# A Hymba-style inference step: RWKV chunk outputs in two rounds, two decoding states moved as whole tiles

## The chip, the core and the metric

One core of a Trainium2 chip runs the whole layer in one launch. The metric is the device time of one execution in microseconds. Every text below uses these names for the engines: PE (TensorE matmul), PEld (its weight loads), DVE (VectorE), ACT (ScalarE), POOL (GpSimd) and SP (SyncE, which here only issues DMAs). ACT and POOL issue DMAs too.

## What is computed

One decoder layer is applied to a prompt of 1024 tokens and to 8 decoding samples of one token each (N = 1032 columns). One input projection feeds four head groups, and a gated output projection and a layer norm close it:

```python
proj = jnp.einsum('ntd,de->nte', x, P['w_in'])
o_A, conv_n, S_A_n = _gdn_branch(...)      # causal convolution, then gated DeltaNet in chunks of 64
o_B, shift_n, S_B_n = _rwkv7_branch(...)   # RWKV-7 time mixing
o_C, k_n, v_n, lf_n = _fox_branch(...)     # attention with forget gates, 4096 cached tokens per sample
o_D, pool_n = _pool_branch(...)            # means over windows of 2, 4, 8 and 16
out = jnp.einsum('nte,ed->ntd', gated, P['w_out'])
y = _layernorm(ALPHA_DN * x + out, P['ln_g'], P['ln_b'])

# B, token by token:
S = S * w_t[:, :, None, :] + s_kk[..., :, None] * (kk_t * a_t)[:, :, None, :] + v_t[..., :, None] * k_t[:, :, None, :]
y_t = jnp.einsum('nhvk,nhk->nhv', S, r_t)
# A and D return the decoding states: the last 3 and the last 15 inputs of each sample
ext = jnp.concatenate([buf, u], axis=1);  new_buf = ext[:, T:]          # A: 3 rows kept
ext = jnp.concatenate([buf, u], axis=1);  new_buf = ext[:, -POOL_BUF:]  # D: 15 rows kept
```

## The kernel before, in words

Every wide product is three f32 matmuls on split operands (`mm3`, L308 to L310). The weights of the input projection (57 tiles of 128 columns) and of the output projection are loaded by ACT's queue as `raw`, split by ACT (`whi`, L302) and DVE (`wlo`, L303), and multiplied into three banks of 344 columns. The projection tiles run one after another on PE. Between them a list of generators ("fillers") is advanced at set rates: preparing the chunk operands, inverting triangular blocks (`invert`, L1176 and L1180), the recurrences, the decoding attention. A scheduler with a timeline of its own then writes the final order of every engine, so a shorter step in one place moves instructions after it. Each engine runs its own list in order.

Three places are touched.

- **`chain_b`** runs the RWKV recurrence over 16 chunks of 64 tokens, as a filler of the last projection tiles. Two heads share the 128 partitions, four such pairs (`hp`) lie side by side. A chunk has four steps on PE: `px` (L1320), `pz` (L1326), `pn` (L1332) and the output `py` (L1340, L1341). L1340 multiplies the old state over all 128 partitions into one half of the output partitions; L1341 adds the products of the chunk over the 64 partitions of one head. Both write 64 x 64 outputs. Each f32 product counts as two PE instructions. ACT then copies `py` into `byT` (L1343) and SP stores it.
- **`branch_d`** (pooling) runs as a filler after both recurrences, while decoding attention streams the cached keys (`dkv<-in_ck`, SP's queue, L924; used by PE at L994). It holds the 15 old rows of 8 samples in `dbf`, in rows of 16, puts the new input in column 15 (L711), sums the last `w` columns (L713) and stores columns 1 to 15 as `obuf` (L725). The same POOL queue stores and loads `dz`, the gate tile (L723, L716), of which there is one buffer.
- **`sample_a`** makes the decoding step of DeltaNet as a filler of the second output pass, beside cached values (`dkv<-in_cv`, L943; used at L1102). It holds the 3 old rows in `scb`, in rows of 4, puts the new input in column 3 (L1524), stores columns 1 to 3 as `oconv` (L1525) and convolves (L1531, L1533). The DMAs between are POOL's. A norm follows: ACT squares `so` into `sqk` (L1561), PE sums it (L1484).

Of the kernel before, what the change touches and what calls it, by code (L numbers as in the profile page):

```python
# [11 lines left out]
ALU = mybir.AluOpType  # L12
AX = mybir.AxisListType
# [166 lines left out]
class Kernel:  # L180
# [502 lines left out]
    def branch_d(self, pool):  # L683
        nc, O, I = self.nc, self.O, self.I
        pw = self.t(pool, [128, 4, 128], "dpw", bufs=1)
        nc.gpsimd.dma_start(pw, I["pw"])
        rc = self.t(pool, [128, 64], "drc", bufs=1)
        nc.gpsimd.dma_start(rc, I["rc"])
        bf = self.t(pool, [128, 4, 8, 16], "dbf", bufs=1)
        nc.gpsimd.dma_start(bf[:, :, :, 0:15], I["dbf"])  # L690
        for gi in range(4):
            w = 2 << gi
            u = self.t(pool, [128, 16 + N], "du", bufs=1)
            nc.gpsimd.memset(u[:, 0:16], 0.0)
            nc.gpsimd.dma_start(u[:, 16:], O["pj"][DU + gi])
            a = self.t(pool, [128, 16 + T], "da", bufs=1)
            b = self.t(pool, [128, 16 + T], "db", bufs=1)
            cur = u
            for s in range(gi + 1):
                d = 1 << s  # L700
                nxt = a if s % 2 == 0 else b
                if s < gi:
                    nc.gpsimd.memset(nxt[:, 0:16], 0.0)
                nc.vector.tensor_tensor(nxt[:, 16:], cur[:, 16:16 + T], cur[:, 16 - d:16 - d + T], op=ALU.add)
                cur = nxt
            nc.vector.tensor_tensor(cur[:, 16:32], cur[:, 16:32], rc[:, 16 * gi:16 * gi + 16], op=ALU.mult)
            yield 1
            po = self.t(pool, [128, 16 + N], "db" if gi % 2 == 0 else "da", bufs=1)[:, :N]
            nc.vector.scalar_tensor_tensor(po[:, :T], cur[:, 16:], 1.0 / w, u[:, 16:16 + T], op0=ALU.mult, op1=ALU.subtract)
            us = u[:, 16 + T:]  # L710
            nc.vector.tensor_copy(bf[:, gi, :, 15], us)  # L711
            sm = self.t(pool, [128, 8], "dsm", bufs=1)
            nc.vector.reduce_sum(sm, bf[:, gi, :, 16 - w:16], axis=AX.X)  # L713
            nc.vector.scalar_tensor_tensor(po[:, T:], sm, 1.0 / w, us, op0=ALU.mult, op1=ALU.subtract)
            z = self.t(pool, [128, N], "dz", bufs=1)
            nc.gpsimd.dma_start(z, O["pj"][DZ + gi])  # L716
            self.silu(z, self.t(pool, [128, 16 + N], "da" if cur is a else "db", bufs=1)[:, :N])
            for g in range(3):
                s = slice(g * G3, g * G3 + G3)
                ps = self.ps("b", (128, G3))  # L720
                nc.tensor.matmul(ps, lhsT=pw[:, gi], rhs=po[:, s], start=True, stop=True)
                nc.vector.scalar_tensor_tensor(z[:, s], ps, self.p("psc", gi), z[:, s], op0=ALU.mult, op1=ALU.mult)
            nc.gpsimd.dma_start(self.G[12 + gi], z)  # L723
            yield 1
        nc.gpsimd.dma_start(O["obuf"], bf[:, :, :, 1:16])  # L725


    def c_values(self, hp):
# [561 lines left out]
    def chain_b(self, **side):  # L1290
        nc, O = self.nc, self.O
        rows = [(slice(0, 64), slice(64, 128)), (slice(64, 128), slice(0, 64))]
        p3 = lambda a: a.rearrange("p (h i) -> p h i", i=64)
        with self.tc.tile_pool(reuse_waits="tile", name="chb", bufs=1, **side) as pool:

            def load(c):
                VZ = self.t(pool, [128, 4, 2, 64], "bvz", bufs=2)
                if c == 16:
                    return None, VZ, None
                op = self.t(pool, [128, 4, 512], "bop", bufs=2)  # L1300
                nc.sync.dma_start(op, self.BOP[c, :, :, 0:512])
                VS = self.t(pool, [128, 4, 2, 64], "bvs", bufs=2)
                for x in (VZ, VS):
                    for h, (_, t) in enumerate(rows):
                        nc.sync.dma_start(x[t, :, h], self.BOP[c, t, :, 512:576])
                return op, VZ, VS
            nxt = load(0)
            for h, (r, _) in enumerate(rows):
                nc.gpsimd.memset(nxt[1][r, :, h], 0.0)
            for c in range(16):  # L1310
                op, VZ, VS = nxt
                nxt = load(c + 1)
                Wv = op[:, :, 0:256].rearrange("p q (h a i) -> p q h a i", h=2, a=2)
                ZP = self.t(pool, [128, 4, 64], "bZP")
                for h, (r, _) in enumerate(rows):
                    nc.gpsimd.tensor_tensor(ZP[r], VZ[r, :, h], self.PC[r, :, c:c + 1].to_broadcast([64, 4, 64]), op=ALU.mult)
                px = self.ps("a", (128, 256))
                for hp in range(4):
                    for h, (r, _) in enumerate(rows):
                        nc.tensor.matmul(px[r, 64 * hp:64 * hp + 64], lhsT=Wv[:, hp, h, 0], rhs=VZ[:, hp, h], start=True, stop=True)  # L1320
                X = self.t(pool, [128, 4, 64], "bX")
                nc.vector.tensor_copy(X, p3(px))
                pz = self.ps("a", (128, 256))
                for hp in range(4):
                    for h, (r, _) in enumerate(rows):
                        nc.tensor.matmul(pz[r, 64 * hp:64 * hp + 64], lhsT=op[r, hp, 448:512], rhs=X[r, hp], start=True, stop=True)  # L1326
                nc.scalar.activation(VS[0:64, :, 0], p3(pz)[0:64], AF.Copy, scale=-1.0)
                nc.vector.tensor_scalar(VS[64:128, :, 1], p3(pz)[64:128], -1.0, None, op0=ALU.mult)
                pn = self.ps("a", (128, 256))
                for hp in range(4):  # L1330
                    for h, (r, _) in enumerate(rows):
                        nc.tensor.matmul(pn[r, 64 * hp:64 * hp + 64], lhsT=op[:, hp, 320 + 64 * h:384 + 64 * h], rhs=VS[:, hp, h],  # L1332
                                         start=True, stop=True)
                for h, (r, _) in enumerate(rows):
                    nc.vector.tensor_tensor(nxt[1][r, :, h], ZP[r], p3(pn)[r], op=ALU.add)
                py = self.ps("a", (128, 256))
                for hp in range(4):
                    o = slice(64 * hp, 64 * hp + 64)
                    for h, (r, _) in enumerate(rows):
                        nc.tensor.matmul(py[r, o], lhsT=VZ[:, hp, h], rhs=Wv[:, hp, h, 1], start=True, stop=False)  # L1340
                        nc.tensor.matmul(py[r, o], lhsT=VS[r, hp, h], rhs=op[r, hp, 256:320], start=False, stop=True)  # L1341
                yT = self.t(pool, [128, 4, 64], "byT", bufs=2)
                nc.scalar.copy(yT, p3(py))  # L1343
                nc.sync.dma_start(self.YB[:, :, 64 * c:64 * c + 64].rearrange("h p t -> p h t"), yT)
                yield True
            for h, (r, _) in enumerate(rows):
                nc.sync.dma_start(O["pBS"][:, r].rearrange("q p d -> p q d"), nxt[1][r, :, h])
# [154 lines left out]
    def sample_a(self, pool):  # L1502
        self.stag = "b"
        nc, I, O = self.nc, self.I, self.O
        pj, v_ = O["pj"], nc.vector
        f = lambda a: a.rearrange("p h b -> p (h b)")
        S = self.t(pool, [128, 4, 8, 64], "sS", bufs=1)
        nc.gpsimd.dma_start(S, I["sA"])
        cb = self.t(pool, [128, 12, 8, 4], "scb", bufs=1)
        nc.gpsimd.dma_start(cb[:, :, :, 0:3], I["cvb"])  # L1510
        xs = self.t(pool, [128, 12, 8], "sxs", bufs=1)
        for s in range(3):
            nc.gpsimd.dma_start(xs[:, 4 * s:4 * s + 4], pj[AT + s:AT + 16:4, :, T:].rearrange("h p b -> p h b"))
# [5 lines left out]
        for hh in range(2):  # L1519
            r = slice(64 * hh, 64 * hh + 64)  # L1520
            nc.gpsimd.dma_start(eg[r], self.gr[hh::2, T:].partition_broadcast(64))
            nc.gpsimd.dma_start(be[r], self.br[hh::2, T:].partition_broadcast(64))
        nc.scalar.activation(eg, eg, AF.Exp)
        v_.tensor_copy(cb[:, :, :, 3], xs)  # L1524
        nc.gpsimd.dma_start(O["oconv"], cb[:, :, :, 1:4])  # L1525
        cw = self.p("conv", 0, n=48).rearrange("p (c k) -> p c k", k=4)
        x = self.t(pool, [128, 12, 8], "sx", bufs=1)
        t = self.t(pool, [128, 12, 8], "st", bufs=1)
        for k in range(4):
            dst = x if k == 0 else t  # L1530
            v_.tensor_tensor(dst, cb[:, :, :, k], cw[:, :, k:k + 1].to_broadcast([128, 12, 8]), op=ALU.mult)  # L1531
            if k:
                v_.tensor_tensor(x, x, t, op=ALU.add)  # L1533
        self.silu(x, t)
        q, k, v = x[:, 0:4], x[:, 4:8], x[:, 8:12]
# [20 lines left out]
        o = self.t(pool, [128, 4, 8], "so", bufs=1)  # L1556
# [370 lines left out]
```

## Time and profile before

| | us |
|---|---|
| median of three runs (2544.55 to 2556.67) | 2548.86 |
| the profiled execution | 2552.96 |
| its span, first to last instruction | 2550.9 |
| PE busy in it | 2393.4 |
| DVE busy | 1371.8 |
| ACT busy | 941.1 |
| POOL busy | 305.7 |

The profile gives, for each engine, the time it was busy, what each wait ended on, and the clock that was granted to PE in a stretch (1.00 is 2.4 GHz, 0.50 is 1.2 GHz). PE instructions overlap in the pipeline, so the distance between the starts of two of them says more than the length of one. DMA share is the mean busy share of the core's 16 DMA engines.

### The profile page before, as it was taken

The numbers are of one execution on the slowest core, as the hardware profiler recorded it, in microseconds if no ns is written. First come the engines' busy times: TensorE is split into PE (matmuls) and PEld (weight loads), VectorE is DVE, ScalarE is ACT, GpSimd is POOL, SyncE is SP. The second block draws the span as 40 slices with busy tenths as digits, with TensorE's granted clock in tenths as the row PEclk, the third lists the DMA queues.
The fourth block names the chain that finished last, engine by engine and source line by source line (L and its number), as shares of the span: only waits on it lengthen the run. The fifth ranks groups of instructions, "written<-read, shape, count | busy, mean of one in ns | idle before, by whom it ended". The sixth has DMA issues, their size and how long they took to land.

```text
span 2550.9 us, 48595 instructions
## 1 busy us (share of the span) xinstructions
PE 2393.4 (94%) x18324; PEld 2101.0 (82%) x18324; DVE 1371.8 (54%) x2674; ACT 941.1 (37%) x1861; POOL 305.7 (12%) x416
## 2 busy tenths in 40 slices
PE   8999999999999999999999997999898799399984
PEld 8999999999979998887788775899655498268984
DVE  4675577687555574212122252555677543264598
ACT  5644444445444441111111121543565563010244
POOL 0000000000000000020111111100222212000065
PEclk9999999999999999889999998999999899799997
DMA  6243334555323357557777887653686767975322
GB/s 205 56 111 94 93 87 113 154 109 117 82 67 88 84 117 171 138 154 217 248 242 263 256 294 201 222 162 87 196 245 207 256 217 206 55 258 174 96 72 83
DMA packets 368740, 401.46 MB, mean 157 GB/s; under 512 B 203853, under 2 KB 227710, under 8 KB 367738
## 3 DMA queue, kind: packets, MB, share of 16 engines
q1 hardware_dynamic: 306418, 262.78, 36.9%
q10 hardware_dynamic: 50056, 101.60, 14.9%
q0 software_dynamic: 12032, 33.99, 4.3%
q8 instruction: 144, 2.36, 0.4%
q14 instruction: 90, 0.74, 0.1%
HBM read 314.56 MB, written 83.62 MB: 156 GB/s over the span
## 4 chain that ended last, share of the span: by engine, by line
PE 57%; DMA 9%; DVE 5%; issue 2%; ACT 1%; SPq 1%; another core or an unknown queue 0%; ACTq 0%; POOL 0%; DVEq 0%; POOLq 0%
PE pj L308 10%; PE pj L309 10%; PE pj L310 10%; PE o L308 4%; PE o L309 4%; PE o L310 3%; PE k L994 3%; DMA raw<-in_wo 3%; PE k L1102 2%; PE a L1341 1%; DMA dkv<-in_ck 1%; PE a L1340 1%; DVE y L1712 1%; DMA dkv<-in_cv 1%; DVE y L1711 1%
## 5 line engine op out<-in xcount | busy, mean ns | idle before, releaser
L308 PE MATMUL pj<-xh,wlo 128*128 128x344 f32 x2688 | 878.8, 328 | 15.8 <-DVE wlo L303 8.2
L309 PE MATMUL pj<-xl,whi 128*128 128x344 f32 x2688 | 875.1, 326 | 0.0
L310 PE MATMUL pj<-xh,whi 128*128 128x344 f32 x2688 | 869.8, 325 | 0.0
L308 PEld LDWEIGHTS pj<-xh,wlo 128*128 128x128 f32 x2688 | 511.4, 190 | 44.4 <-issue 18.2
L310 PEld LDWEIGHTS pj<-xh,whi 128*128 128x128 f32 x2688 | 511.7, 191 | 19.3 <-issue 16.1
L309 PEld LDWEIGHTS pj<-xl,whi 128*128 128x128 f32 x2688 | 512.0, 190 | 18.0 <-issue 12.3
L302 ACT CAST whi<-raw 128x256 fp32r<-128x256 f32 (+1 forms) x504 | 212.9, 424 | 772.9 <-PE pj L310 513.7
L303 DVE TENSOR_TENSOR wlo<-raw,whi 128x256 fp32r<-128x256 f32 (+1 forms) x504 | 225.3, 449 | 421.8 <-ACT whi L302 411.5
L308 PE MATMUL o<-gh,wlo 128*128 128x344 f32 x576 | 186.3, 328 | 4.7 <-ACT gh L1656 4.7
L309 PE MATMUL o<-gl,whi 128*128 128x344 f32 x576 | 186.8, 324 | 0.0
L310 PE MATMUL o<-gh,whi 128*128 128x344 f32 x576 | 186.2, 323 | 0.0
L308 PEld LDWEIGHTS o<-gh,wlo 128*128 128x128 f32 x576 | 108.7, 190 | 28.9 <-DVE y L1681 10.2
L309 PEld LDWEIGHTS o<-gl,whi 128*128 128x128 f32 x576 | 109.9, 191 | 4.7 <-issue 4.2
L310 PEld LDWEIGHTS o<-gh,whi 128*128 128x128 f32 x576 | 109.6, 190 | 3.3 <-issue 3.2
L994 PE MATMUL k<-dkv,dqb 128*32 128x256 f32 x1024 | 93.2, 400 | 17.4 <-DMA dkv<-in_ck 17.1
L365 ACT ACTIVATE stg<-pj 128x344 f32<-128x344 f32 x168 | 75.0, 457 | 90.4 <-PE pj L310 89.4
L1681 DVE TENSOR_TENSOR y<-y,o 128x344 f32<-128x344 f32 x96 | 48.1, 509 | 78.2 <-PE o L310 78.1
L1102 PE MATMUL k<-dkv,dpT 128*8 128x512 f32 x512 | 69.7, 620 | 4.6 <-DMA dkv<-in_cv 4.5
L858 DVE TENSOR_TENSOR cpl<-cpt,cph 128x512 fp32r<-128x512 f32 (+1 forms) x96 | 62.7, 667 | 19.5 <-ACT cph L857 18.9
L308 PE MATMUL o<-gh,wkl 128*128 128x392 f32 (+2 forms) x192 | 63.8, 332 | 0.5 <-DVE wkl L303 0.5
L994 PEld LDWEIGHTS k<-dkv,dqb 128*32 128x32 f32 x1024 | 27.7, 109 | 43.8 <-issue 30.6
L310 PE MATMUL o<-gh,wkh 128*128 128x392 f32 (+2 forms) x192 | 63.8, 332 | 0.0
(590 smaller groups left out, 3553.2 us busy)
## 6 DMA issues: line engine op xcount, KB each, us to landing
dkv<-in_ck SPq DMA_DIRECT2D x256, 256.0 KB
dkv<-in_cv SPq DMA_DIRECT2D x256, 256.0 KB
raw<-in_w ACTq DMA_DIRECT2D x228, 256.0 KB
out_pj<-stg ACTq DMA_DIRECT2D x33, 516.0 KB
bop<-bop SPq DMA_DIRECT2D x16, 1024.0 KB
raw<-in_wo ACTq DMA_DIRECT2D x64, 256.0 KB
aop<-aop SPq DMA_DIRECT2D x16, 768.0 KB
aop<-aost SPq DMA_DIRECT2D x40, 256.0 KB
```

The lines of the kernel that those rows point to most:

```text
L302: nc.scalar.copy(hi, raw)
L303: nc.vector.tensor_tensor(lo, raw, hi.bitcast(F32), op=ALU.subtract)
L308: nc.tensor.matmul(ps, lhsT=wlo, rhs=xh, start=start, stop=False)
L309: nc.tensor.matmul(ps, lhsT=whi, rhs=xl, start=False, stop=False)
L310: self.last = nc.tensor.matmul(ps, lhsT=whi, rhs=xh, start=False, stop=stop).ins
L365: self.nc.scalar.activation(dst[:, g * G3:g * G3 + G3], ps[g], func)
L858: nc.vector.tensor_tensor(pl[:, off:], pt[:, off:], ph[:, off:].bitcast(F32), op=ALU.subtract)
L994: nc.tensor.matmul(ps[32 * hp:32 * hp + 32], lhsT=qb[:, hp, b], rhs=kt[:, :, hp], start=b == 0, stop=b == 7)
L1102: mm = lambda i: nc.tensor.matmul(po[32 * i:32 * i + 8], lhsT=pTv[:, c, :, 4 * bg + i], rhs=t[i // 2][:, i % 2], start=False, stop=c == 31)
L1340: nc.tensor.matmul(py[r, o], lhsT=VZ[:, hp, h], rhs=Wv[:, hp, h, 1], start=True, stop=False)
L1341: nc.tensor.matmul(py[r, o], lhsT=VS[r, hp, h], rhs=op[r, hp, 256:320], start=False, stop=True)
L1681: nc.vector.tensor_tensor(y[:, s], y[:, s], ps[g], op=ALU.add)
```

## The change

In `chain_b` the two products of a chunk's output no longer alternate: first the eight products over 128 partitions, one for each `hp` and head, then the eight over 64. The first product of the chunk alone starts a fresh accumulation, the last alone ends it. In `branch_d` and `sample_a` the old state is loaded into a tile with no gaps, and the new state is made in a second tile by copies on DVE, so that both DMAs move a contiguous run per partition: 480 elements (obuf) and 288 (oconv) where single runs of 15 and of 3 elements stood. The window of 16 then needs one extra addition.

```diff
-        bf = self.t(pool, [128, 4, 8, 16], "dbf", bufs=1)
-        nc.gpsimd.dma_start(bf[:, :, :, 0:15], I["dbf"])
+        bf, bn = (self.t(pool, [128, 4, 8, 15], x, bufs=1) for x in ("dbf", "dbn"))
+        nc.gpsimd.dma_start(bf, I["dbf"])
+        nc.vector.tensor_copy(bn[:, :, :, 0:14], bf[:, :, :, 1:15])
...
-            nc.vector.tensor_copy(bf[:, gi, :, 15], us)
+            nc.vector.tensor_copy(bn[:, gi, :, 14], us)
...
-            nc.vector.reduce_sum(sm, bf[:, gi, :, 16 - w:16], axis=AX.X)
+            nc.vector.reduce_sum(sm, bn[:, gi, :, 15 - w:15] if w < 16 else bn[:, gi], axis=AX.X)
+            if w == 16:
+                nc.vector.tensor_tensor(sm, sm, bf[:, gi, :, 0], op=ALU.add)
...
-        nc.gpsimd.dma_start(O["obuf"], bf[:, :, :, 1:16])
+        nc.gpsimd.dma_start(O["obuf"], bn)
...
                 for hp in range(4):
-                    o = slice(64 * hp, 64 * hp + 64)
                     for h, (r, _) in enumerate(rows):
-                        nc.tensor.matmul(py[r, o], lhsT=VZ[:, hp, h], rhs=Wv[:, hp, h, 1], start=True, stop=False)
-                        nc.tensor.matmul(py[r, o], lhsT=VS[r, hp, h], rhs=op[r, hp, 256:320], start=False, stop=True)
+                        nc.tensor.matmul(py[r, 64 * hp:64 * hp + 64], lhsT=VZ[:, hp, h], rhs=Wv[:, hp, h, 1], start=hp == 0, stop=False)
+                for hp in range(4):
+                    for h, (r, _) in enumerate(rows):
+                        nc.tensor.matmul(py[r, 64 * hp:64 * hp + 64], lhsT=VS[r, hp, h], rhs=op[r, hp, 256:320], start=False, stop=hp == 3)
...
-        cb = self.t(pool, [128, 12, 8, 4], "scb", bufs=1)
-        nc.gpsimd.dma_start(cb[:, :, :, 0:3], I["cvb"])
+        cb, cn = (self.t(pool, [128, 12, 8, 3], x, bufs=1) for x in ("scb", "scn"))
+        nc.gpsimd.dma_start(cb, I["cvb"])
...
-        v_.tensor_copy(cb[:, :, :, 3], xs)
-        nc.gpsimd.dma_start(O["oconv"], cb[:, :, :, 1:4])
+        v_.tensor_copy(cn[:, :, :, 0:2], cb[:, :, :, 1:3])
+        v_.tensor_copy(cn[:, :, :, 2], xs)
+        nc.gpsimd.dma_start(O["oconv"], cn)
...
-            v_.tensor_tensor(dst, cb[:, :, :, k], cw[:, :, k:k + 1].to_broadcast([128, 12, 8]), op=ALU.mult)
+            v_.tensor_tensor(dst, cb[:, :, :, k] if k < 3 else xs, cw[:, :, k:k + 1].to_broadcast([128, 12, 8]), op=ALU.mult)
```

The first chunk output stands so in PE's list before (a row here is one product; its output tile, its operands, its output's shape):

```order
L1332 MATMUL a_10394<-bvs_10354,bop_10352 64x64 x7
L1340 MATMUL a_10405<-bop_10352,bvz_10351 64x64
L1341 MATMUL a_10405<-bop_10352,bvs_10354 64x64
L1340 MATMUL a_10405<-bop_10352,bvz_10351 64x64
L1341 MATMUL a_10405<-bop_10352,bvs_10354 64x64
...
L1176 MATMUL k_10871<-ivT_10864,ivD_10866 32x32 x12
L1320 MATMUL a_10498<-bvz_10361,bop_10362 64x64 x8
```

The pair of L1340 and L1341 stands there eight times. The same place in PE's list now (the lines are three to six further down in the file):

```order
L1335 MATMUL a_10394<-bvs_10354,bop_10352 64x64 x7
L1343 MATMUL a_10405<-bop_10352,bvz_10351 64x64 x8
L1346 MATMUL a_10405<-bop_10352,bvs_10354 64x64 x8
L1179 MATMUL k_10871<-ivT_10864,ivD_10866 32x32 x12
L1323 MATMUL a_10498<-bvz_10361,bop_10362 64x64 x8
```

Fifteen changes between the two kinds of product have become one; what stands around the step is the same. After this chunk the scheduler's order differs on every engine: with the matmuls of the projections counted, the last key product of decoding (L994) comes 200 of them earlier in PE's list.

At the end of the third pooling window POOL's list was this (a row is a memory set or a DMA, with its destination's or source's shape as the DMA sees it):

```order
L695 DMA du_18720<-out_pj 128x1032
L703 MEMSET da_18723 128x16
L725 DMA out_obuf<-dbf_17807 4096x1x15
L703 MEMSET db_18724 128x16
L723 DMA gated<-dz_18553 128x1032
L703 MEMSET da_18723 128x16
L716 DMA dz_18885<-out_pj 128x1032
```

And now:

```order
L696 DMA du_18722<-out_pj 128x1032
L728 DMA out_obuf<-dbn_17808 128x480
L704 MEMSET da_18725 128x16
L704 MEMSET db_18726 128x16
L726 DMA gated<-dz_18555 128x1032
L704 MEMSET da_18725 128x16
L1004 DMA sco<-dso_17597 128x512
L977 MEMSET dcum_18323 128x513
L719 DMA dz_18888<-out_pj 128x1032
```

The store keeps its place ahead of the gate's store; its 4096 runs have become 128, and a store of decoding scores (`sco<-dso`) has come in ahead of the last gate's load. In DVE's list, the copy that the change adds in `branch_d` stands here now:

```order
L303 TENSOR_TENSOR wlo_17562<-raw_17443,whi_17561 128x256
L303 TENSOR_TENSOR wlo_17700<-raw_17443,whi_17699 128x256
L691 COPY dbn_17808<-dbf_17807 128x32x14
L1002 SCALAR_TENSOR_TENSOR dso_16939<-k_16940,dcum_16925 128x256
L705 TENSOR_TENSOR da_17814<-du_17811 128x1024
L712 COPY dbn_17808<-du_17811 128x8
L303 TENSOR_TENSOR wlo_17724<-raw_17541,whi_17723 128x256
```

It stands ahead of the reading of a bank of decoding scores (`dso`, L999 before) and of a weight split.

## Rows read from the trace of the kernel before

**Rows 1.** The page's head and part 1: busy us, share, instructions.

```profile
span 2550.9 us, 48595 instructions
...
PE 2393.4 (94%) x18324; PEld 2101.0 (82%) x18324; DVE 1371.8 (54%) x2674; ACT 941.1 (37%) x1861; POOL 305.7 (12%) x416
```

**Rows 2.** Busy time by stretch: us, PE, PEld, DVE, ACT, POOL, clock, DMA share, GB/s.

```profile
600.00:650.00 50.00, 49.26 (x580) 47.24 (x579) 24.58 (x49) 20.53 (x40) 5.32 (x9) 1.00 0.61 130
961.00:1243.00 282.00, 280.36 (x2762) 235.87 (x2760) 76.31 (x187) 44.69 (x106) 40.76 (x69) 0.92 0.67 176
1243.00:1440.00 197.00, 193.56 (x2294) 156.92 (x2291) 42.39 (x99) 25.98 (x65) 25.73 (x45) 0.99 0.77 253
1440.00:1530.00 90.00, 84.53 (x651) 65.53 (x644) 40.34 (x71) 21.00 (x38) 19.49 (x40) 1.00 0.89 289
1530.00:1570.00 40.00, 24.55 (x152) 18.52 (x154) 12.32 (x18) 6.00 (x11) 2.96 (x5) 0.79 0.80 162
...
2190.00:2240.00 50.00, 6.82 (x35) 6.13 (x35) 4.33 (x15) 2.56 (x6) 0.57 (x1) 0.56 0.94 60
2240.00:2400.00 160.00, 160.00 (x981) 138.87 (x980) 87.76 (x135) 24.69 (x34) 1.52 (x3) 1.00 0.56 187
```

**Rows 3.** DMA issues: queue, count, KB each, us to landing.

```profile
gated<-pz POOLq DMA_DIRECT2D x16, 256.0 KB, 4.9
...
out_obuf<-dbf POOLq DMA_DIRECT2D x1, 240.0 KB, 21.9
...
out_oconv<-scb POOLq DMA_DIRECT2D x1, 144.0 KB, 67.6
```

**Rows 4.** ACT's timeline, 2178 to 2236 us, with idle time and its releaser.

```profile
2222.60 0.62 ACT L302 CAST whi<-raw 128x512 fp32r<-128x512 f32 x1 [43.15 <-DMA raw<-in_wo]
```

**Rows 5.** PE's timeline, 2188 to 2240 us.

```profile
2236.00 0.64 PE L1484 MATMUL b<-sqk,b64r 128*128 128x32 f32 x2 [43.18 <-ACT sqk L1561]
```

**Rows 6.** PE's timeline in one chunk: start us, us, line, out<-in, shape, count.

```profile
1045.23 0.49 PE L308 MATMUL pj<-xh,wlo 128*128 128x344 f32 x1
1045.52 0.49 PE L309 MATMUL pj<-xl,whi 128*128 128x344 f32 x1
...
1049.51 0.68 PE L1326 MATMUL a<-bX,bop 64*64 64x64 f32 x16
1050.12 0.42 PE L308 MATMUL pj<-xh,wlo 128*128 128x344 f32 x1
...
1053.14 0.69 PE L1332 MATMUL a<-bvs,bop 128*64 128x64 f32 x16
1053.65 0.28 PE L1340 MATMUL a<-bop,bvz 128*64 128x64 f32 x2
1053.86 0.33 PE L1341 MATMUL a<-bop,bvs 64*64 64x64 f32 x2
...
1057.71 0.42 PE L308 MATMUL pj<-xh,wlo 128*128 128x344 f32 x1
1057.97 0.31 PE L309 MATMUL pj<-xl,whi 128*128 128x344 f32 x1
1058.12 0.32 PE L310 MATMUL pj<-xh,whi 128*128 128x344 f32 x1
```

**Rows 7.** SP's waits, 2100 to 2260 us: total us, times, longest.

```profile
SPq L943 <- DMA dkv<-in_cv: 31.5, 4, 17.5
```

**Rows 8.** Waits of all engines, 1530 to 1575 us.

```profile
POOL dz L716 <- DMA gated<-dz: 21.9, 1, 21.9
...
PE k L994 <- DMA dkv<-in_ck: 9.5, 2, 9.3
...
PE pj L308 <- ACT stg L365: 5.9, 1, 5.9
```

**Rows 9.** DVE's timeline, 2150 to 2175 us.

```profile
2167.42 0.25 DVE L1524 COPY scb<-sxs 128x96 f32<-128x96 f32 x1
```

**Rows 10.** The page's part 5: count, busy us, mean ns, idle before and releaser.

```profile
L994 PE MATMUL k<-dkv,dqb 128*32 128x256 f32 x1024 | 93.2, 400 | 17.4 <-DMA dkv<-in_ck 17.1
```

## The prediction

> **What bounds the kernel now.** I read the page's busy times first: PE is busy for 2393.4 of 2550.9 us, the next engine for 54% [rows 1]. So PE's list is the path, and a change pays where it shortens a step on PE or takes away a stretch in which PE waits. The table of busy time by stretch says where each of these is [rows 2]. From 961 to 1243 us, where the RWKV recurrence runs, PE is busy for 280.36 of 282 us: the time there is what PE's instructions take, and its clock was 0.92. At 1530 to 1570 PE works only 24.55 of 40 us, and at 2190 to 2240 only 6.82 of 50: two holes. In the second the DMA engines are 0.94 busy and move 60 GB/s, against 253 GB/s at a share of 0.77 in a normal stretch: they work on something with tiny pieces. The list of DMA issues names it: `oconv` took 67.6 us to land, `obuf` 21.9, while a transfer of 256 KB on the same queue takes 4.9 [rows 3]. The timelines of ACT and PE then show who waited behind it [rows 4, 5].
>
> **The chunk outputs.** In the timeline of one chunk [rows 6] the output starts at 1053.65 with a pair of instructions over 128 partitions (one product), then a pair over 64, and so on; the next matmul of the projection starts at 1057.71. That is 4.06 us for 16 products, 0.254 each. Sixteen products' worth of instructions of one kind cost far less: the 16 instructions of L1332 (128 partitions) take from 1053.14 to 1053.65, 0.51 us, so 0.032 each; the 16 of L1326 (64 partitions) take from 1049.51 to 1050.12, 0.61 us with the change to the projection's matmuls behind them. A product is two instructions, so 0.254 - 0.064 = 0.19 us of each is the change of kind. Now there is one such change inside the step: 0.51 + 0.19 + 0.61 = 1.31 us. The step shrinks by 2.75 us. The loop has 16 chunks: 44 us. All of it lies on PE's list, which hardly waits there [rows 2], so I take it in full. Bounds: 49 us (16 x (4.06 - 1.02)) if the change of kind inside costs nothing, and 12 if the products of the second round go one by one: a pair of L1341 is 0.33 us long, eight of them 2.64, the step 0.51 + 0.19 + 2.64 = 3.3. Against that stands L1326, in which two heads use different halves of the partitions and write one bank, and yet the 16 start 32 ns apart [rows 6].
>
> The lower end is what a rule makes of it. The Trainium skill (TensorEngine Tiling (Array Packing), Gotcha 1: PSUM Pressure) says that different row tiles cannot access the same PSUM bank at the same time; by it the second round would go one by one. The trace doesn't agree in L1326.
>
> **The clock.** From 961 to 1243 the granted clock is 0.92, that is 0.08 x 2 x 282 = 45 us at the lower level, 1.2 GHz [rows 2]. At that level the projection's matmuls start 0.29 us apart instead of 0.15 to 0.16 [rows 6], so some 22.5 us are lost. The drops come behind chunk outputs that small inversion products follow; one stands at 1045. From 600 to 650 us inversions run without chunk outputs, and the clock is 1.00 [rows 2]. Bounds 0 and 22.5; I take 16, nearer to the second row, because the small products before and behind the output stay.
>
> How the clock is set is told by the Trainium skill (TensorE: Matmul & The Clock Gate, Part 1) as activity releasing a default throttle. By it a shorter stretch of thin work can only help; it does not say whether 1.31 us is short enough.
>
> **The convolution's states.** PE waits 43.18 us for `sqk` [rows 5]; ACT stood 43.15 us before a weight piece `raw` that was in flight behind the `oconv` store [rows 4]. The store has 12288 runs of 12 bytes, 768 per DMA engine; 67.6 / 768 is 88 ns a run (`obuf`: 4096 runs, 256 per engine, 21.9 / 256 = 86 ns, so the price is by the run). With 128 runs, 8 per engine, it should land like the 256 KB transfer, in some 5 us. What is late next: the cached values, for which SP waited at most 17.5 us in this region [rows 7]; 43 - 17.5 = 25.5 is the lower bound. Upper bound 46, with the clock that was 0.56 when PE resumed. After the hole PE is busy for all of 160 us at a DMA share of 0.56 [rows 2], so there is room: I take 43.
>
> **The pooling states.** Behind `obuf` on the queue stands the gate's store, POOL waits 21.9 us for it before it may load the next gate into the single buffer `dz`, ACT sits in the gate's function and not on the projection's bank, and PE waits 5.9 us there; before that PE waits 9.3 us for a page of keys in flight at the same time [rows 8]. The hole is 40 - 24.55 = 15.45 us, and the clock of 0.79 costs a few more. Bounds: 6 (the page stays late, only the bank's wait goes) and 20; I take 16. In POOL's new order a store of scores comes in ahead of the last gate's load; it waits for DVE, not for the hole, and I count nothing for it.
>
> **What is added.** A copy of 448 elements and one of 192 per partition, and one addition of 8, on DVE. A copy of 96 took 0.25 us [rows 9]; by size 448 is at most 1.2. DVE is free 46% of the time and PE's own work covers it: 0. The copy in `branch_d` is also a new wait, for the load of `dbf`. Behind it on DVE stand the reading of a score bank (`dso`) and a weight split, and PE's key products wait for that bank. The load is issued ahead of `du`, for which DVE waited before at nearly the same place, so I take 0, and up to 5 us (one landing) if it comes late.
>
> **What is given back.** The key pages are 64 MB that must pass while the recurrences and the pooling run. With PE faster there, the DMA share rises. From 1440 to 1530 us it was 0.89 and PE idled 6% (5.47 of 90); from 1243 to 1440 it was 0.77 and PE idled 1.7% [rows 2]. If the roughly 300 us with pages before 1440 become like the former, some 4 to 5% of it, 14 us, go. I take 8, with bounds 0 and 25.
>
> **Sum.** 44 + 16 + 43 + 16 - 8 = 111. The profiled execution took 2552.96, its span 2550.9, so 2.1 us lie around it; 2550.9 - 111 + 2.1 = 2442. It is 4.1 us above the median of the runs shown, 2548.86, from which the same sum gives 2438. I predict 2440.
>
> **Rivals.**
> - *Pages bind.* The time saved up to 1570 us is where decoding keys stream in, and PE waits for pages instead: the 7 or 8 chunk outputs that run beside the pages (22 us) and half of the pooling's hole (8) come back as waits. For it: 0.89 share at 289 GB/s with waits already. Against it: the two holes themselves, in which pages crawled, go. Time: 2440 + 30 = 2470.
> - *Clock stays low and the second hole half remains.* The small products around the outputs alone keep the clock where it is (+16), and cached values replace the weights as what PE waits for (+17.5). For it: SP's 17.5 us. Against: the clock of 1.00 at 600 us. Time 2474.
> - *The second round runs one by one*: 12 of the 44 us are gained, and with a step of 3.3 us most of the clock's 16 isn't (+13). Against it: L1326 [rows 6]. Time 2440 + 32 + 13 = 2485. (It is what the rule of TensorEngine Tiling in the Trainium skill would make of the step.)
> - *Slower than before.* The scheduler has moved PE's list from the first chunk on. If the new order sets key products ahead of pages that aren't there yet, each such wait holds the whole list; the longest now is 9.3 us [rows 8]. The key products are 1024 instructions, issued eight at a time, 128 groups, and wait 17.4 us in all now [rows 10]. It takes 12 waits of the longest kind (111 / 9.3) more before the kernel is slower than before; at 16 it is 2440 + 149 = 2589. For it: the last key product comes 200 projection matmuls earlier. Against it: the pages' issue moves with it, and two such waits are all that there is now.
>
> **Chances.** The forecast 0.78, pages 0.10, clock and hole 0.06, one by one 0.03, slower 0.02, and 0.01 for nothing changed. The forecast's own range, with its bounds added as independent ones, is 2418 to 2465. For 8 in 10 over all I take 2412 to 2482: it has the first two rivals within it, and below it the upper bounds of all four terms together (49 + 22 + 46 + 20 = 137, 2414). Within 0.5% (13 us, about what can be told from no change here) lies hardly anything: faster 0.97, same 0.01, slower 0.02.
>
> **What would show it.** In the new trace: the chunk output from its first product to the next other matmul takes about 1.3 us, not 4.06; the clock from 960 to the end of the RWKV recurrence is above 0.97; `oconv` and `obuf` land within 10 us; no wait of PE over 15 us stands beside `sample_a`, and the gate's load in `branch_d` follows its store within 10 us. I am wrong if PE's waits for key pages, 1200 to 1600 us, come to more than 30 us in all, if the clock stays at 0.92, or if the hole beside `sample_a` stays above 20 us.

## The result, and the profile after

The changed kernel took 2429.35 us, median of four runs (2426.1 to 2435.51), against 2547.77 for the kernel before on the same chip: a ratio of 0.953 with an interval of 0.950 to 0.957. Two repetitions on other chips gave 0.949 (0.945 to 0.954) and 0.948 (0.945 to 0.951). The forecast was 2440, so the change was worth about 119 us where 111 were forecast, and by the ratios of the two repetitions 130 and 133.

The profiled execution took 2431.75. Head and part 1 of its page, which answer to [rows 1]:

```profile
span 2430.0 us, 48607 instructions
...
PE 2330.0 (96%) x18324; PEld 2055.6 (85%) x18324; DVE 1371.7 (56%) x2677; ACT 940.3 (39%) x1861; POOL 298.8 (12%) x416
```

The span is 120.9 us shorter. PE's busy time fell by 63.4 (2393.4 to 2330.0), its idle time by 57.5 (157.5 to 100.0). These two halves are what the steps of the prediction have to fill. First the busy half: PE's timeline of one chunk output (start us, us, line, out<-in, shape, count), as in [rows 6]:

```profile
1078.64 0.33 PE L1335 MATMUL a<-bvs,bop 128*64 128x64 f32 x2
1078.90 0.24 PE L1179 MATMUL k<-ivT,ivD 32*32 32x32 f32 x2
1079.07 0.62 PE L1335 MATMUL a<-bvs,bop 128*64 128x64 f32 x13
1079.48 0.22 PE L1343 MATMUL a<-bop,bvz 128*64 128x64 f32 x1
...
1079.54 0.68 PE L1343 MATMUL a<-bop,bvz 128*64 128x64 f32 x15
1080.15 0.68 PE L1346 MATMUL a<-bop,bvs 64*64 64x64 f32 x16
1080.76 0.81 PE L1179 MATMUL k<-ivT,ivD 32*32 32x32 f32 x20
```

From the first product at 1079.48 to the next other matmul at 1080.76 are 1.28 us; 4.06 stood there before. Twelve of the sixteen chunks show 1.28, the others 2.0 to 3.8, because the next matmul had to wait (three times for a key page, 0.8 to 2.5 us). Then the stretches (us, PE, PEld, DVE, ACT, POOL, clock, DMA share, GB/s), which answer to [rows 2] in the same order of work; the second and the third are the RWKV recurrence and what follows it:

```profile
600.00:650.00 50.00, 48.96 (x526) 47.09 (x525) 25.28 (x51) 19.79 (x38) 5.11 (x8) 0.90 0.56 127
965.00:1196.00 231.00, 218.69 (x2727) 187.41 (x2727) 76.77 (x187) 45.08 (x107) 42.85 (x71) 0.97 0.81 217
1196.00:1380.00 184.00, 182.73 (x2206) 146.01 (x2205) 39.74 (x93) 24.05 (x60) 25.98 (x44) 1.00 0.85 279
...
1460.00:1500.00 40.00, 38.80 (x286) 29.57 (x285) 22.43 (x36) 10.74 (x18) 8.62 (x19) 1.00 0.90 296
2050.00:2250.00 200.00, 200.00 (x1244) 168.97 (x1243) 106.00 (x190) 33.64 (x62) 10.46 (x17) 1.00 0.65 210
```

The recurrence runs at 0.97 instead of 0.92. But PE now idles there: 12.3 of 231 us, where 1.6 of 282 stood before [rows 2]. More than half of it is a wait that the stretch didn't have before, the key pages (us in total, times, longest; 965 to 1196 us):

```profile
PE k L997 <- DMA dkv<-in_ck: 6.9, 7, 2.5
```

Both holes are gone: PE works 38.80 of the 40 us in which `obuf` is stored (1460 to 1500), and all of the 200 us around `oconv`. The DMA issues (count, KB each, us to landing) and PE's waits (us in total, times, longest) say why; they answer to [rows 3] and to [rows 5, 8, 10]:

```profile
gated<-pz POOLq DMA_DIRECT2D x16, 256.0 KB, 3.8
...
out_obuf<-dbn POOLq DMA_DIRECT2D x1, 240.0 KB, 3.7
...
out_oconv<-scn POOLq DMA_DIRECT2D x1, 144.0 KB, 5.2
```

```profile
PE o L1732 <- DVE y L1736: 14.7, 6, 5.3
PE k L997 <- DMA dkv<-in_ck: 12.9, 13, 2.8
...
PE v L870 <- DVE cpl L861: 6.4, 4, 4.4
...
PE pj L308 <- ACT stg L365: 1.3, 3, 0.5
...
PE k L1105 <- DMA dkv<-in_cv: 0.4, 1, 0.4
```

No wait for `sqk` is left (43.2 before), and no wait for a key page is longer than 2.8 us. The largest in the list is the tail's, which the kernel before had too.

### The profile page after: what moved, and what is told of

It reads as the page before. It is cut to its first block, busy times and chain, and to the rows that moved or that the text cites. A ratio compares the mean times of both kernels' runs of the same rounds, so it can differ in the third digit from the quotient of the medians.

```text
span 2430.0 us, 48607 instructions
## 1 busy us (share of the span) xinstructions
PE 2330.0 (96%) x18324; PEld 2055.6 (85%) x18324; DVE 1371.7 (56%) x2677; ACT 940.3 (39%) x1861; POOL 298.8 (12%) x416
## 5 line engine op out<-in xcount | busy, mean ns | idle before, releaser
L997 PE MATMUL k<-dkv,dqb 128*32 128x256 f32 x1024 | 90.6, 394 | 13.4 <-DMA dkv<-in_ck 12.9
L861 DVE TENSOR_TENSOR cpl<-cpt,cph 128x512 fp32r<-128x512 f32 (+1 forms) x96 | 61.7, 660 | 16.2 <-ACT cph L860 15.4
L309 PE MATMUL o<-gl,wkh 128*128 128x392 f32 (+2 forms) x192 | 63.3, 330 | 0.0
```

Of the source, the lines that this page charges most:

```text
L309: nc.tensor.matmul(ps, lhsT=whi, rhs=xl, start=False, stop=False)
L861: nc.vector.tensor_tensor(pl[:, off:], pt[:, off:], ph[:, off:].bitcast(F32), op=ALU.subtract)
L997: nc.tensor.matmul(ps[32 * hp:32 * hp + 32], lhsT=qb[:, hp, b], rhs=kt[:, :, hp], start=b == 0, stop=b == 7)
```

## The experiments

Every ratio is to the kernel before, from runs on one chip; the median of the kernel before on it stands beside the first of each set. Lines are those of each variant's own file.

**The three parts alone.** e1_rounds is the kernel before with only the hunk of `chain_b`:

```diff
+                        nc.tensor.matmul(py[r, 64 * hp:64 * hp + 64], lhsT=VZ[:, hp, h], rhs=Wv[:, hp, h, 1], start=hp == 0, stop=False)
+                for hp in range(4):
+                    for h, (r, _) in enumerate(rows):
+                        nc.tensor.matmul(py[r, 64 * hp:64 * hp + 64], lhsT=VS[r, hp, h], rhs=op[r, hp, 256:320], start=False, stop=hp == 3)
```

In each chunk the first product of each head starts the accumulation and the last of each head ends it.

> The kernel before with the chunk outputs in two rounds, and nothing else. Theory: the step takes 1.28 us as in the changed kernel (4.06 before), 44 us for 16 chunks, all of it on PE's path, and the clock between the start and the end of the RWKV recurrence rises from 0.92 to 0.96 or more, 10 to 20 us: 2485 to 2495, ratio 0.975 to 0.979, with both holes still there. Rival (the clock has nothing to do with the step): 44 us alone, 2504, ratio 0.983, clock at 0.92. Rival (key pages bind): PE's waits for pages grow by more than 15 us and the ratio is above 0.985.

Measured: 2501.42 us (before: 2561.59), ratio 0.978 (0.974 to 0.982), about 56 us. PE is busy for 2329.8 us, just as in the full change, and the step is 1.28. One stretch and two waits of it:

```profile
961.00:1184.00 223.00, 210.69 (x2713) 180.67 (x2711) 75.55 (x184) 43.37 (x103) 42.54 (x69) 1.00 0.83 224
```

```profile
PE b L1486 <- ACT sqk L1563: 35.8, 1, 35.8
PE k L994 <- DMA dkv<-in_ck: 23.4, 15, 9.3
```

So the fall in PE's busy time is this part's, clock included. The hole beside `sample_a` stays, and the waits for key pages grow from 17.1 to 23.4: that is the giving back, 6 us of it at the keys. PE's whole idle time is 164.3 us (2494.1 - 2329.8), 6.8 more than before.

e2_conv is the kernel before with only the hunks of `sample_a`:

```diff
-        cb = self.t(pool, [128, 12, 8, 4], "scb", bufs=1)
-        nc.gpsimd.dma_start(cb[:, :, :, 0:3], I["cvb"])
+        cb, cn = (self.t(pool, [128, 12, 8, 3], x, bufs=1) for x in ("scb", "scn"))
+        nc.gpsimd.dma_start(cb, I["cvb"])
...
-        nc.gpsimd.dma_start(O["oconv"], cb[:, :, :, 1:4])
+        nc.gpsimd.dma_start(O["oconv"], cn)
```

> The kernel before with the convolution's state moved as whole tiles, and nothing else. Theory: the store of oconv lands in under 10 us, PE's wait of 43 us for sqk goes, and with it most of the low clock behind it: 43 to 46 us, 2502 to 2505, ratio 0.982 to 0.983; the step of the chunk outputs stays at 4.06 us. Rival (cached values or the next weight piece take the store's place): 25 us, ratio 0.990, and a wait of 15 us or more beside the decoding step.

Measured: 2509.84, ratio 0.980 (0.976 to 0.984), about 52 us (41 to 62). `oconv` lands in 5.2 us and PE never waits for `sqk`. The step is still 4.06 and the clock beside it no better:

```profile
961.00:1256.00 295.00, 294.34 (x2776) 246.01 (x2775) 77.37 (x188) 45.72 (x109) 41.95 (x71) 0.88 0.64 169
```

e3_pool is the kernel before with only the hunks of `branch_d`:

```diff
-        bf = self.t(pool, [128, 4, 8, 16], "dbf", bufs=1)
-        nc.gpsimd.dma_start(bf[:, :, :, 0:15], I["dbf"])
+        bf, bn = (self.t(pool, [128, 4, 8, 15], x, bufs=1) for x in ("dbf", "dbn"))
+        nc.gpsimd.dma_start(bf, I["dbf"])
...
-        nc.gpsimd.dma_start(O["obuf"], bf[:, :, :, 1:16])
+        nc.gpsimd.dma_start(O["obuf"], bn)
```

> The kernel before with the pooling state moved as whole tiles, and nothing else. Theory: obuf lands in under 6 us, the gate's load follows its store within 10 us, the hole of 15 us goes with its low clock: 12 to 18 us, ratio 0.993 to 0.995. Rival (key pages that were late there are late elsewhere): under 6 us, ratio above 0.998, and PE's waits for pages stay at 17 us in all or grow.

Measured: 2533.47, ratio 0.990 (0.986 to 0.994), about 26 us (17 to 35) where the forecast had 16 and the expectation 12 to 18. Two stretches, the same as two of [rows 2], and two of its groups (count, busy us, mean ns, idle before and releaser):

```profile
1440.00:1530.00 90.00, 88.69 (x745) 68.73 (x743) 39.10 (x69) 22.19 (x40) 18.84 (x41) 1.00 0.88 290
1530.00:1570.00 40.00, 39.12 (x292) 29.78 (x293) 18.67 (x34) 8.16 (x15) 9.03 (x18) 1.00 0.90 292
```

```profile
L997 PE MATMUL k<-dkv,dqb 128*32 128x256 f32 x1024 | 95.3, 408 | 3.5 <-DMA dkv<-in_ck 3.5
L1105 PE MATMUL k<-dkv,dpT 128*8 128x512 f32 x512 | 70.6, 628 | 46.1 <-DMA dkv<-in_cv 46.1
```

The hole at 1530 closes (24.55 to 39.12 us of work in 40), and the 90 us before it gain 4.2 us too (84.53 to 88.69): the key pages hardly make PE wait any more, 3.5 us against 17.4 [rows 10]. The second line is the hole beside `sample_a`, still there. In this run PE waits behind the same store at another instruction, for cached values and not for `sqk`.

**One kind change, or two products into one place?** In the kernel before, each pair also wrote the same place twice in a row. e4_apart changes kind seven times but never writes the place that was written last:

```diff
+                each = [(hp, h, r) for hp in range(4) for h, (r, _) in enumerate(rows)]
+                for i in range(12):
+                    if i < 8:
+                        wide(*each[i])
+                    if i >= 4:
+                        half(*each[i - 4])
```

> The changed kernel, but with the two kinds of product alternating again, each half product four places behind its full one, so that neighbours write different places of the bank (eight changes of kind for each direction in the middle, 9 in all instead of 15 or 1). Theory (a change of kind costs 0.19 us, wherever the product writes): the order is four full, then full and half in turn four times, then four half, 8 changes; with 2 instructions a product at 0.032 us the step is 1.02 + 8 x 0.19 + 0.1 = about 2.6 us. Rival (what costs is that a product adds to the place that the one before it has just written): no such neighbours are left, the step stays at 1.3 us.

Measured: 2443.15 in one run. PE's timeline of one output (`wide` is L1341, `half` L1342):

```profile
1001.07 0.22 PE L1341 MATMUL a<-bop,bvz 128*64 128x64 f32 x1
...
1001.13 0.46 PE L1341 MATMUL a<-bop,bvz 128*64 128x64 f32 x9
1001.51 0.32 PE L1342 MATMUL a<-bop,bvs 64*64 64x64 f32 x2
1001.77 0.33 PE L1341 MATMUL a<-bop,bvz 128*64 128x64 f32 x2
1002.03 0.33 PE L1342 MATMUL a<-bop,bvs 64*64 64x64 f32 x2
...
1003.05 0.56 PE L1342 MATMUL a<-bop,bvs 64*64 64x64 f32 x10
1003.54 0.94 PE L1179 MATMUL k<-ivT,ivD 32*32 32x32 f32 x24
```

Every pair still takes 0.26 us though its neighbours write elsewhere, and the step takes 2.47 (1001.07 to 1003.54), with seven changes by the timeline (the expectation counted one or two more). The price is the change of kind: (4.06 - 1.28) / 14 = 0.199 us for each over the whole range, and (2.47 - 1.28) / 6 = 0.198 for these.

e5_four has three changes, in groups of four products:

```diff
+                for q in (each[:4], each[4:]):
+                    for x in q:
+                        wide(*x)
+                    for x in q:
+                        half(*x)
```

> The changed kernel, but the chunk's output comes in four groups instead of two: four products over 128 partitions, four over 64, four over 128, four over 64. Three changes of kind inside the step instead of one. Theory (0.199 us for each change, linear in their number): the step takes 1.28 + 2 x 0.199 = 1.68 us. Rival (the price belongs to two products that follow each other into the same place of the bank, or only the first few changes are dear): 1.28 to 1.4 us. The granted clock in the stretch of the RWKV recurrence lies between that with one change (0.97 to 1.00) and that with seven (0.97) if it follows their number; the time of one look 2431 + 16 x 0.4 = about 2437.

Measured: 2441.37 in one run; the step takes 1.57 or 1.58 us in twelve chunks of sixteen:

```profile
1001.75 0.22 PE L1341 MATMUL a<-bop,bvz 128*64 128x64 f32 x1
...
1001.81 0.45 PE L1341 MATMUL a<-bop,bvz 128*64 128x64 f32 x7
1002.19 0.45 PE L1342 MATMUL a<-bop,bvs 64*64 64x64 f32 x8
1002.57 0.45 PE L1341 MATMUL a<-bop,bvz 128*64 128x64 f32 x8
1002.95 0.45 PE L1342 MATMUL a<-bop,bvs 64*64 64x64 f32 x8
1003.33 0.94 PE L1179 MATMUL k<-ivT,ivD 32*32 32x32 f32 x24
```

That is 0.15 for each of the two added changes, above the rival's 1.28 to 1.4 and below the 1.68 that 0.199 each would give. So the number of changes sets the step, and 0.2 us is their price where the groups are as short as a pair; between longer groups it is less.

**Load or store?** These are the changed kernel with one transfer put back. e6_store stores `oconv` from rows of 4 again (12288 runs of 12 bytes) and loads it whole:

```diff
-        cb, cn = (self.t(pool, [128, 12, 8, 3], x, bufs=1) for x in ("scb", "scn"))
+        cb = self.t(pool, [128, 12, 8, 3], "scb", bufs=1)
+        cn = self.t(pool, [128, 12, 8, 4], "scn", bufs=1)
...
-        nc.gpsimd.dma_start(O["oconv"], cn)
+        nc.gpsimd.dma_start(O["oconv"], cn[:, :, :, 0:3])
```

> The changed kernel, but the new convolution state is kept in rows of 4 and stored as 12288 runs of 12 bytes again; its load stays whole. Theory (the store's runs, at 87 ns each on a DMA engine, make the hole): it lands in 60 to 70 us, PE waits 30 to 45 us once beside the decoding step, and the kernel is that much slower than the changed one: ratio to before about 0.970 where the changed one has 0.953. Rival (the load's runs make the hole, the store is only seen because it is queued behind them): it lands in under 20 us, no such wait, 0.953.

Measured: 2474.31 (before: 2565.51; the changed kernel in the same set, after_again: 2430.3), ratio 0.966 (0.962 to 0.970). The store's row and PE's longest wait:

```profile
out_oconv<-scn POOLq DMA_DIRECT2D x1, 144.0 KB, 66.0
```

```profile
PE k L1105 <- DMA dkv<-in_cv: 39.3, 1, 39.3
```

e7_load is the reverse, a whole store and a load into rows of 4:

```diff
-        nc.gpsimd.dma_start(cb, I["cvb"])
+        cb = self.t(pool, [128, 12, 8, 4], "scb", bufs=1)
+        nc.gpsimd.dma_start(cb[:, :, :, 0:3], I["cvb"])
```

> The changed kernel, but the old convolution state is loaded into rows of 4, as 12288 runs of 12 bytes; its store stays whole. Theory (the store makes the hole): the load lands in 15 to 18 us instead of 8.7, off PE's path, and the ratio to before is that of the changed kernel, 0.953 to 0.956. Rival (the load makes it): PE waits 20 us or more beside the decoding step, 0.963 or more.

Measured: 2429.89, ratio 0.949 (0.945 to 0.953), the same as the changed kernel beside it:

```profile
scb<-in_cvb POOLq DMA_DIRECT2D x1, 144.0 KB, 17.1
out_oconv<-scn POOLq DMA_DIRECT2D x1, 144.0 KB, 6.2
```

The store alone makes the hole, 44 us of it. The load with the same runs costs a quarter as long on the queue, and no time that can be told.

e8_bufstore puts back the store of `obuf` alone:

```diff
-        bf, bn = (self.t(pool, [128, 4, 8, 15], x, bufs=1) for x in ("dbf", "dbn"))
+        bf = self.t(pool, [128, 4, 8, 15], "dbf", bufs=1)
+        bp = self.t(pool, [128, 4, 8, 16], "dbn", bufs=1)
+        bn = bp[:, :, :, 0:15]
```

> The changed kernel, but the new pooling state is kept in rows of 16 and stored as 4096 runs of 60 bytes again; its load stays whole. Theory (the store's runs make the hole, at 86 ns each): it lands in 20 to 23 us, the gate's store behind it in as long, and PE waits 10 to 15 us there: ratio to before 0.957 to 0.959. Rival (the load of 60-byte rows, or the order that came with the change, is what gave the 25 us that this part alone gained): under 5 us, 0.953 to 0.955.

Measured: 2450.8, ratio 0.956 (0.951 to 0.960), by the medians 20 us slower than the changed kernel beside it. The intervals of the two ratios overlap, but the slowest of the changed kernel's four runs in this set (2437.62) is faster than the fastest of these four (2441.95). The store's row, a wait and a stretch:

```profile
out_obuf<-dbn POOLq DMA_DIRECT2D x1, 240.0 KB, 21.9
```

```profile
PE k L999 <- DMA dkv<-in_ck: 23.1, 17, 10.2
```

```profile
1440.00:1500.00 60.00, 48.20 (x336) 36.78 (x336) 27.11 (x43) 12.87 (x23) 10.59 (x22) 0.89 0.90 234
```

The hole is back (11.8 us in these 60), the clock is at 0.89 in it, and waits for key pages rise from 12.9 to 23.1. So some 20 of the 26 us that the pooling part gave alone hang on the store; the rest is within the noise. The way through the gate is hardly seen here: a store of scores that waits for DVE has come in ahead of the gate's load, POOL waits 0.5 us for the gate's own store, and PE's longest wait for the bank (`stg`) is 1.3. The longest wait for a page, 10.2, is nearly the whole hole.

```profile
1488.56 0.53 POOL L721 DMA_DIRECT2D dz<-out_pj  x1 [0.51 <-DMA gated<-dz]
```

**after_again**, the changed kernel beside those three:

> The changed kernel itself, on the same chip as the three before it, to compare with: ratio to before 0.950 to 0.957. If the three parts' gains simply added (56, 52 and 26 us) it would be 0.948.

Measured: 2430.3, ratio 0.949 (0.945 to 0.954), where the added gains would make 0.948.

**Can two more changes of kind go?** In the changed kernel the step L1335 is split, its first product apart from the other seven, as the first rows of the timeline above show. e10_pn takes the heads in reverse there:

```diff
-                    for h, (r, _) in enumerate(rows):
+                    for h, (r, _) in reversed(list(enumerate(rows))):
```

> The changed kernel, but the eight products of the chunk's new values (L1335, 64 partitions of the weights) are issued for the other head first. In the changed kernel's order the first of the eight stands alone, with a projection matmul between it and the other seven, in all 16 chunks (32 rows of it in the order, 16 rows now). Theory (a change between kinds of product costs 0.2 us wherever it stands): two changes less in each chunk, 2 x 0.2 x 16 = 6.4 us less time on PE, PE busy about 2324 instead of 2330, the ratio to the kernel before about 0.2 to 0.3% lower than that of the changed kernel (0.949 to 0.953), so 0.947 to 0.951. Rival (the price is not the change but the output step's own pairs of instructions, and a single matmul in between is overlapped): nothing is gained, PE busy 2329 to 2331, and because the first product now waits for the head whose values DVE makes later, up to 0.5 us a chunk is lost, 8 us.

Measured: 2427.8 (before: 2558.21), ratio 0.949 (0.947 to 0.952). PE is busy for 2316.9 us, less than the theory's 2324, but idle for 106.3 (2423.2 - 2316.9). Between sets the time can't be told from the changed kernel's, so both ran once more on one chip, e11_after and e12_pn:

> The changed kernel again, beside e12_pn on one chip, as the base for comparing the two: about 2430 us, ratio to the kernel before 0.949 to 0.954.

> The kernel of e10_pn again, on one chip with e11_after. Theory (two changes of kind less per chunk, L1335's busy time 16.1 to 11.0 us in its profile): 5 to 8 us below e11_after, PE busy lower by as much. Rival (the gain on PE comes back as waits elsewhere): equal times within 2 us, with idle time of PE longer by 5 us or more.

Measured: 2429.55 and 2430.73 (before: 2560.98), ratios 0.948 (0.945 to 0.951) and 0.948 (0.945 to 0.951): the same. In e12_pn the step is whole and L1335's busy time falls from 16.3 to 11.0 us, PE's from 2325.6 to 2321.5. But PE's idle time rises from 98.1 (2423.7 - 2325.6) to 110.3 (2431.8 - 2321.5). One stretch of each shows a place, first e11_after, then e12_pn:

```profile
1400.00:1500.00 100.00, 96.47 (x699) 74.22 (x701) 51.98 (x89) 25.25 (x44) 18.47 (x41) 1.00 0.88 293
```

```profile
1400.00:1500.00 100.00, 90.47 (x637) 70.20 (x636) 46.98 (x81) 20.42 (x36) 16.75 (x38) 0.95 0.77 254
```

The pages stream less densely there in the order that the scheduler made of the edit, and PE's waits for keys from 1200 to 1500 us are 10.6 instead of 5.6. Over the whole span the waits for keys hardly differ (15.0 and 14.2); those for cached values do, 7.3 against 1.2, and 4.3 in e10_pn. The rival of e12_pn holds: what PE's list gained came back as idle time, in both profiles of the edit (106.3 and 110.3, against 98.1 to 100.0 in the three of the changed kernel). How much came back isn't settled to a few us: the profiled run of e12_pn is the slowest of its five (2433.63) and that of e11_after the fastest (2425.47), and a gain of 2 or 3 us would not show in medians of runs that spread over 5 and 10. Whether another order would keep the 4 us was not tried. No version here can be told to beat the changed kernel.

## Why the prediction was right

The mechanisms of its main terms are in the traces, and no rival came true; one term was mis-sized, and some readings were wrong without moving the sum. By its steps:

- **Chunk outputs, 44 us.** 16 x (4.06 - 1.28) = 44.5. The second round doesn't take 0.33 us a pair: L1346's sixteen instructions take 0.61 us, with the row halves writing one bank in turn. Whether two halves ever write at the same moment no run shows: these sixteen take no less than the 0.51 us of L1332's [rows 6], which use all rows. So the rows don't contradict the rule of the Trainium skill that was weighed (TensorEngine Tiling (Array Packing), Gotcha 1: PSUM Pressure), though the prediction reads L1326 so; what they rule out is the rival's price, 0.33 us a pair. Another rule of that page (Key Properties), that changing the tiling mode drains the engine, agrees with the price on each change in e4_apart and e5_four; it gives no price itself, and the runs give 0.15 to 0.2 us. That PE's list "hardly waits there" held for the kernel before alone; PE's busy time in the recurrence fell by 61.7 us and its idle time rose by 10.7, so the stretch gained 51 (282 to 231).
- **Clock, 16 us.** What PE's busy time lost beyond the step is 63.4 - 44.5 = 19 us. The rows of the recurrence agree: 0.97 over 231 us is 0.03 x 2 x 231 = 14 us at the lower level, some 7 lost, against 22.5 before, so 15.5 regained. In e1_rounds, where this hunk alone was changed, it was 1.00, so the edit raises the clock; by which of its features isn't shown. "Above 0.97" was just missed in the profiled run of the changed kernel. The kernel before also stood well in the profile that was read: e2_conv and e3_pool, which still have the old output, show 0.88 there, 0.12 x 295 = 35 us lost. That the larger gain of the repetitions comes from this isn't shown.
- **Convolution's states, 43 us.** 43.2 us of waiting went and nothing came late after it (PE's wait for cached values is 0.4 us). Putting the store back costs 44. Alone the part gave 52, with an interval that holds 43.
- **Pooling's states, 16 us, mis-sized.** Alone it gave 26 (17 to 35), and by its store alone some 20. The step counted the hole at 1530 and the clock in it. It did not count that PE's waits for pages outside the hole would fall as well: in e3_pool the 90 us before it gain 4.2 us, and PE's wait for `cpl`, 12.3 us before, is 5.6. Why that last one fell isn't settled, as it fell in e2_conv too (6.9). Of the two ways from the store to PE that the prediction gives, e8_bufstore bears out the page (10.2 us); the bank behind the gate has 5.9 us in the kernel before [rows 8] and no run of its own. The queue behaves as forecast: the gate's load follows its store by 5 us, where POOL waited 21.9 [rows 8]. Rows of POOL's timeline after:

```profile
1469.94 0.55 POOL L728 DMA_DIRECT2D out_obuf<-dbn  x1 [7.01 <-DVE dbn L712]
...
1478.36 0.54 POOL L726 DMA_DIRECT2D gated<-dz  x1 [0.74 <-DVE dz L725]
...
1483.39 0.53 POOL L719 DMA_DIRECT2D dz<-out_pj  x1 [0.81 <-DMA gated<-dz]
```

- **What is added, 0.** The two copies take 0.4 and 0.3 us on DVE (groups of the changed kernel: count, busy us, mean ns, idle before):

```profile
L691 DVE COPY dbn<-dbf 128x448 f32<-128x448 f32 x1 | 0.4, 394 | 2.0 <-DMA dbf<-in_dbf 2.0
...
L1529 DVE COPY scn<-scb 128x192 f32<-128x192 f32 x1 | 0.3, 323 | 4.0 <-DMA scb<-in_cvb 4.0
```

  DVE's wait for the load of `dbf` is 2.0 us, and the profile has no wait that ended on either copy.
- **Given back, -8 us, right in kind and covered.** From e3_pool to the full change PE's waits for keys rise from 3.5 to 12.9 (12.0 and 14.2 in the profiles of the repetitions), 9.4 us: that is what faster outputs give back at the keys (6.3 in e1_rounds, beside the slow stores). In the sum the pooling's gain at the same pages lies over it, so the total falls from 17.1 to 12.9. The rival that pages bind counted on 30 us; from 1200 to 1600 us the waits for keys are 6.0, where more than 30 was to show the forecast wrong. The rival that it gets slower needed twelve waits of 9.3 more; there are thirteen in all, the longest 2.8. Its "two such waits are all that there is now" is misread: [rows 8] has two waits of 9.5 us in all, so one of 9.3 and one of 0.2.
- **The range.** 2418 to 2465 doesn't come out of the bounds added as independent ones: their squares give about 12 us below the 2440 and 44 above, 2428 to 2484. The measured 2429 lies inside either, near the lower end; the bounds allowed pooling 20 us at most, and alone it gave 26.

The idle half, 57.5 us, is nearly the sum of five waits: 43.2 (`sqk`), 6.4 (`stg`, 7.7 to 1.3), 5.9 (`cpl`), 4.2 (keys) and 4.1 (cached values), less a net 6 that small waits elsewhere added. Forecast were 43 + 16 - 8 = 51 for it and 60 for the busy half, so the 10 us that the span gained more are 6.5 of waits and 3.4 of work. The three parts alone add up to 134 us, the full change measures 119 to 133 by its ratios: within the intervals nothing is lost between them.

## What to carry to other kernels

Group products by the partitions that they span: on PE's list a change of kind cost 0.15 to 0.2 us, as much as two to three products of one kind (0.064 each), and its price is read from the starts of neighbours in the timeline. Look for stores with tiny runs by their landing time, and ask who uses the DMA engines during it: the wait stood on an engine and a queue that had nothing to do with the store. When a change frees time on the bound engine, check by idle time, not by busy time, whether the end moves: e12_pn saved 4 us of work and no time that its runs show.

## What the runs showed beside

- A store costs by its runs: 12288 of 12 bytes took 66.0 to 69.9 us in e1_rounds, e3_pool and e6_store, 4096 of 60 bytes 21.4 to 22.3, so 84 to 91 ns a run at both sizes, if the runs are shared evenly among 16 engines. A load of the same 12-byte runs took 16.4 to 17.4, 21 to 23 ns a run.
- The granted clock in the recurrence was 0.88 to 0.92 with fifteen changes of kind in a chunk's output (before, e2_conv, e3_pool) and 0.97 to 1.00 with one. The 0.97 with seven (e4_apart) and the 0.98 with three (e5_four) lie within the range of one, so that the clock follows the number of changes isn't shown; only the fifteen stand apart. Over the whole span the kernel before had a mean clock of 0.961 in the profile that the forecast rests on, and 0.953 to 0.963 in its 38 later runs: that profile was a good one for the kernel before.
- It also moves where nothing was changed: from 600 to 650 us it was 0.90 in the profiled run of the changed kernel and 1.00 before [rows 2], and over 600 to 960 us it was 0.99 to 1.00 in all runs. A few us between two profiles are worth no explanation.
